# 32 unused bytes behind each tile of the split activations in a diffusion trunk layer

## The chip, the core and the metric

The kernel runs on one core of one Trainium2 chip. The metric is the time of one execution on the device in microseconds (us). The kernel before takes 2071.98 us, the median of two runs (2070.9 and 2073.06).

The core has engines that run side by side: TensorE (PE; its weight loads are shown apart as PEld), VectorE (DVE), ScalarE (ACT), GpSimd (POOL) and SyncE (SP), whose queue here issues most of the transfers. TensorE multiplies a stationary operand, which a weight load brings in first, with a moving operand that streams past it column by column. Both operands come from SBUF, the on-chip memory of 128 partitions; a tile's address is the same byte offset in each partition. Products land in PSUM, from where the other engines read them.

## The reference

One layer of a diffusion backbone for 128 context tokens and 256 latent tokens, d = 2048, float32:

```python
def trunk_layer(x, cond, lw, attend):
    sh1, sc1, g1, sh2, sc2, g2 = modulation(cond, w_mod_l, b_mod_l)
    h = rms_norm(x, n1) * (1 + sc1) + sh1
    q, k, v, u = project_in(h, w_in_l, qg_l, kg_l)      # 2048 x 4096
    attn = attend(q, k, v)
    x = x + g1 * token_mixing(h, attn, u, w_na_proj_l, w_fnet_proj_l, w_gate_l, w_o_l)
    h2 = rms_norm(x, n2) * (1 + sc2) + sh2
    x = x + g2 * swiglu(h2, w_gu_l, w_down_l)           # 2048 x 11264, 5632 x 2048
    return x, k, v

def token_mixing(h, attn, u, w_na_proj, w_fnet_proj, w_gate, w_o):
    na = attn.reshape(b, t, D_NA) @ w_na_proj
    fn = fourier_mix(u) @ w_fnet_proj
    g_na, g_fn = jnp.split(jax.nn.sigmoid(h @ w_gate), 2, axis=-1)
    return (g_na * na + g_fn * fn) @ w_o
```

Context tokens attend to context tokens; latent tokens attend to a window of their grid and to a cached context. The outputs are the new tokens of both kinds and the context's keys and values.

## The kernel before, in words

**Precision by three products.** Every float32 operand x is split into two tiles of a faster float32 form: H, a rounded copy (ScalarE, line 137), and L = x - H (VectorE, line 138). `mm3` (lines 140 to 143) then adds three matmuls into one PSUM tile: aH with bH (line 141), aH with bL (line 142) and aL with bH (line 143). The first argument is stationary and the second moves.

**Weights** come in units of 256 rows by 512 columns (`load_unit`, line 178) in one long fixed order, `units`. `next_unit` splits the unit ahead into `wh` and `wl`, tiles of [128, 2, 512], so 4096 bytes in a partition, three buffers each in `wpool`. A matmul reads either 512 columns of such a tile as the moving operand or a slice of 128 columns (512 bytes) as the stationary one.

**Activations** lie transposed, with channels on the partitions and the 384 tokens along the free dimension: a tile of [128, 384] float32, 1536 bytes. `hH[kt]` and `hL[kt]`, kt = 0 to 15, are allocated by `new_h` in the pool `hpool`, one tag for each, in the order H0, L0, H1, L1 and so on. The same 32 places are used three times: for the modulated input h, for the mixed branches (`mixH`, `mixL`), and for the second normalised input. The feed-forward part is done in pieces of eight (at last four) tiles of hidden channels; `cH[i]` and `cL[i]`, i = 0 to 7, are the split products of silu(g) and a, of the same size, in the pool `actp`.

**The stages**, in order of time: the input projection (h stationary, weights move, 512 columns), with the modulation vectors computed alongside; the gates (weights stationary, h moves, 384 columns), with the Fourier branch and attention run in small steps between; the two branch projections (weights stationary; the branch tiles `aH`, `aL`, `fH`, `fL` move); the output projection (the mixed tiles stationary, 512 columns); then six times gate-and-up (h moves, 384 columns) and down (c stationary, 512 columns). Work that runs alongside is held in generators (`Paced`) that a fixed number of steps is taken from at each weight unit, so that the order on each engine is fixed by the program. The last results are added up and stored at the end of the last down projection.

**Two places that the prediction looks at besides.** In the Fourier branch, `channels` multiplies tables of cosines and sines (stationary) with the sums over positions, tiles of [128, 2, 2, 194] (`sums`), 388 moving columns in two groups of 194. In attention, `values` multiplies the values (stationary) with the transposed probabilities `pt`, 512 moving columns in two runs of 256, and then 256 for the context.

**Where tiles lie.** In the pool `small` one tile, `pad`, of 480 bytes is allocated and never used. In the program before, `hH`, `hL`, `cH`, `cL`, `wh`, `wl`, `aH`, `aL`, `fH` and `fL` all begin at 288 modulo 512.

Of the kernel before, what the change touches and what calls it, by code (L numbers as in the profile page):

```python
# [13 lines left out]
F32 = mybir.dt.float32  # L14
F32R = mybir.dt.float32r
# [4 lines left out]
P = 128  # L20
# [9 lines left out]
TOK = CTX + LAT  # L30
# [65 lines left out]
def trunk_kernel(ctx: ExitStack, tc: tile.TileContext, io: dict):  # L96
# [25 lines left out]
    hpool = ctx.enter_context(tc.tile_pool(name="hpool", bufs=1))  # L122
# [9 lines left out]
    def nm(s):  # L132
        return f"{s}{next(ids)}"


    def split(H, L, x):
        nc.scalar.copy(H, x)  # L137
        nc.vector.tensor_sub(L, x, fr(H))  # L138

    def mm3(out, aH, aL, bH, bL, start, stop):  # L140
        nc.tensor.matmul(out, aH, bH, start=start, stop=False)  # L141
        nc.tensor.matmul(out, aH, bL, start=False, stop=False)  # L142
        nc.tensor.matmul(out, aL, bH, start=False, stop=stop)  # L143
# [58 lines left out]
    def next_unit(late=False):  # L202

        for p in front:
            p.tick()
        if not late:
            split_unit()
        for p in front + behind:
            p.tick()
        loads.more()  # L210
        return ready.popleft()
# [12 lines left out]
    hH = [None] * KT  # L224
    hL = [None] * KT

    def new_h(kt):
        hH[kt] = hpool.tile([P, TOK], F32R, tag=f"tH{kt}", name=nm(f"hH{kt}_"))
        hL[kt] = hpool.tile([P, TOK], F32R, tag=f"tL{kt}", name=nm(f"hL{kt}_"))
        return hH[kt], hL[kt]  # L230

    s_qkvu = [dram.tile([P, NT, CH], F32, tag=f"sq{i}", name=f"s_qkvu{i}") for i in range(8)]
# [28 lines left out]
    with ExitStack() as ph:  # L261
# [12 lines left out]
        def acc_tile():  # L274

            return next(ring)()
# [146 lines left out]
        with ExitStack() as pha:  # L423
# [90 lines left out]
            def modulate(kt):  # L514
                o = at_tile()
                for t in range(NT):
                    x = xc[kt // 4][:, t, kt % 4 * P : (kt % 4 + 1) * P]
                    if kt < 4:
                        nc.tensor.matmul(o[:, t * P : (t + 1) * P], x, diag[:, t], start=True, stop=True)
                    else:  # L520
                        nc.tensor.transpose(o[:, t * P : (t + 1) * P], x, ident)
                H, L = new_h(kt)
                f = tmp.tile([P, TOK], F32, tag="hf", name=nm("hf"))
                if kt == 0:
                    for cnd, sl in ((0, slice(0, CTX)), (1, slice(CTX, TOK))):
                        sc, sh = (m[0][:, kt, cnd : cnd + 1] for m in (msc, msh))
                        nc.vector.tensor_scalar(f[:, sl], o[:, sl], sc, sh, op0=ALU.mult, op1=ALU.add)
                        nc.scalar.copy(H[:, sl], f[:, sl])
                        nc.vector.tensor_sub(L[:, sl], f[:, sl], fr(H[:, sl]))
                    return  # L530
                for cnd, sl in ((0, slice(0, CTX)), (1, slice(CTX, TOK))):
                    nc.scalar.activation(
                        out=f[:, sl], in_=o[:, sl], func=AF.Identity,
                        scale=msc[0][:, kt, cnd : cnd + 1], bias=msh[0][:, kt, cnd : cnd + 1],
                    )
                split(H, L, f)
# [476 lines left out]
        def mixed(f4, gl):  # L1013
            for f in range(4):
                kt = f4 * 4 + f
                mixH[kt], mixL[kt] = new_h(kt)
                nc.vector.tensor_add(gl[0][:, f], gl[0][:, f], gl[1][:, f])
                split(mixH[kt], mixL[kt], gl[0][:, f])
                if f == 3:
                    gates.more()  # L1020
                    gates.more()
                yield
# [156 lines left out]
    def split_act(i, sg, cH, cL):  # L1179
        for f in range(4):  # L1180
            split(cH[i + f], cL[i + f], sg[:, f])
            yield

    def gated():

        rows_until(5)
        phr.close()
        pool = phr.enter_context(tc.tile_pool(name="gbp", bufs=1, side="right"))
        for cc in range(4):
            yield from load_rows(pool, 5, cc)  # L1190
        for cc in range(4):
            for t in range(NT):
                v = facc[cc][:, t]
                nc.vector.tensor_mul(v, v, gb[cc][:, min(t, 1)])
                nc.vector.tensor_add(x2[cc][:, t], x2[cc][:, t], v)
                yield

    f0 = 0
    for part, nf in enumerate(FF_PARTS):
        last = part == len(FF_PARTS) - 1  # L1200
        if last:
            behind.append(Paced(gated(), 1.5))
        cH = [None] * nf
        cL = [None] * nf
        for c4 in range(nf // 4):
            for half in (1, 0):
                po = [acc_tile() for _ in range(4)]
                for u in range(0, KT, 2):
                    wH, wL = next_unit()
                    if u == KT - 2 and facc is None:  # L1210
                        norm.drain()
                        rows.rate = RATES[4]
                        pho.close()
                        actp = phf.enter_context(tc.tile_pool(name="actp", bufs=1))
                        facc = [actp.tile([P, NT, CH], F32, tag=f"fa{i}", name=f"facc{i}") for i in range(4)]
                        ftmp = phf.enter_context(tc.tile_pool(name="tmpf", bufs=2))
                    for f in range(4):
                        s = slice(f * P, (f + 1) * P)
                        for kk in range(2):
                            k = u + kk  # L1220
                            mm3(po[f][:, :TOK], wH[:, kk, s], wL[:, kk, s], hH[k], hL[k], k == 0, k == KT - 1)
                        if u < KT - 2:
                            continue
                        if half:
                            if f == 0:
                                sg = ftmp.tile([P, 4, TOK], F32, tag="sg", name=nm("sg"))
                            nc.scalar.activation(out=sg[:, f], in_=po[f][:, :TOK], func=AF.Silu)
                        else:
                            i = c4 * 4 + f
                            nc.vector.tensor_mul(sg[:, f], sg[:, f], po[f][:, :TOK])  # L1230
                            cH[i] = actp.tile([P, TOK], F32R, tag=f"cH{i}", name=nm("cH"))
                            cL[i] = actp.tile([P, TOK], F32R, tag=f"cL{i}", name=nm("cL"))
                            if nf == 4:
                                split(cH[i], cL[i], sg[:, f])
            if nf > 4:
                behind.append(Paced(split_act(c4 * 4, sg, cH, cL), 2))
        for cc in range(4):
            po = [acc_tile() for _ in range(NT)]
            for u in range(0, nf, 2):
                wH, wL = next_unit()  # L1240
                for t in range(NT):
                    sl = slice(t * P, (t + 1) * P)
                    for kk in range(2):
                        k = u + kk
                        mm3(po[t], cH[k][:, sl], cL[k][:, sl], wH[:, kk], wL[:, kk], k == 0, k == nf - 1)
                    if u < nf - 2:
                        continue
                    if part == 0:
                        nc.scalar.copy(facc[cc][:, t], po[t])
                    elif not last:  # L1250
                        nc.vector.tensor_add(facc[cc][:, t], facc[cc][:, t], po[t])
                    else:
                        d = ftmp.tile([P, CH], F32, tag="d", bufs=1, name=nm("d"))
                        nc.vector.tensor_mul(d, po[t], gb[cc][:, min(t, 1)])
                        nc.vector.tensor_add(x2[cc][:, t], x2[cc][:, t], d)
                        y = yp if t == 0 else ys[(t - 1) * P : t * P]
                        nc.sync.dma_start(y[:, cc * CH : (cc + 1) * CH], x2[cc][:, t])
        f0 += nf
# [52 lines left out]
```

## Time and profile before

| | before |
|---|---|
| median of the runs | 2071.98 us (2070.9 to 2073.06) |
| the profiled execution's own time | 2074.18 us |
| its span, first to last instruction | 2072.4 us |
| mean granted TensorE clock | 0.997 |
| instructions | 27373 |
| moved by DMA | 390.45 MB, mean 188 GB/s |

The profile comes from one execution. Its rows of groups give line, engine, operation, the tile written and the tiles read, the shape, the number of instructions, then after the bar the busy time in us and the mean of one in ns, and then the idle time just before them with what ended it. A row of the list of waits gives who waited for whom, then the total in us, the number of times and the longest. A row of the timeline gives the start in us from the span's start, the duration in us, and the instruction. Matmuls are pipelined and their ends are modelled: their durations overlap, so that the distance from one start to the next, and not the duration, is what a matmul costs when TensorE is the limit.

### The profile page before, as it was taken

What the parts mean: (1) busy time and instruction counts of PE and PEld (TensorE: products, weight loads), DVE (VectorE), ACT (ScalarE), POOL (GpSimd) and SP (SyncE); (2) the same over time, 40 slices, a digit from 0 to 9 for tenths busy, and PEclk for the clock granted to TensorE, in tenths of its full rate; (3) what the DMA queues carried; (4) which work ended last, traced back from release to release, by engine and by line L of the source; (5) the groups of instructions that cost most, each with busy time, mean ns of one, the idle gap of its engine ahead of it and who ended that gap; (6) DMA issues with size and microseconds to landing.
All of it is one profiled execution on the core that took longest, in us unless ns stands there. A gap on an engine that the chain in (4) does not pass through costs nothing.

```text
span 2072.4 us, 27373 instructions
## 1 busy us (share of the span) xinstructions
PE 2036.6 (98%) x10963; PEld 1847.0 (89%) x10963; DVE 1209.9 (58%) x1418; ACT 756.2 (36%) x1146; POOL 58.0 (3%) x101
## 2 busy tenths in 40 slices
PE   6999999999999999998999999999999999999999
PEld 4668888999999999887998899899989998999897
DVE  4634899687885787765554444544454434333456
ACT  5323232456665433334433332223222232223222
POOL 3000000000001000001000000000000000000000
PEclk9999999999999999999999999999999999999999
DMA  9886878677674766654455454455454444444453
GB/s 336 286 321 211 295 254 309 211 212 235 212 218 152 261 230 212 235 191 128 150 161 159 157 162 148 138 162 157 158 158 137 123 132 124 130 125 130 128 167 122
DMA packets 219999, 390.45 MB, mean 188 GB/s; under 512 B 28080, under 2 KB 64960, under 8 KB 219872
## 3 DMA queue, kind: packets, MB, share of 16 engines
q1 hardware_dynamic: 212704, 382.13, 58.1%
q10 hardware_dynamic: 4672, 6.31, 0.8%
q8 instruction: 86, 1.41, 0.3%
q0 software_dynamic: 2496, 0.27, 0.1%
q14 instruction: 41, 0.34, 0.0%
HBM read 371.81 MB, written 20.51 MB: 189 GB/s over the span
## 4 chain that ended last, share of the span: by engine, by line
PE 94%; DVE 2%; DMA 1%; ACT 1%; issue 1%; SPq 1%; ACTq 0%; DVEq 0%
PE mm L141 19%; PE mm L142 19%; PE mm L143 19%; PE at L143 11%; PE at L141 11%; PE at L142 11%; PE md L390 1%; DMA wm<-in_w_mod 1%; DVE accr L314 1%; PE at L850 1%; PE at L918 1%; DVE wl L138 1%; DMA xc<-in_x_sample 0%; SPq L368 0%; PE md L324 0%
## 5 line engine op out<-in xcount | busy, mean ns | idle before, releaser
L138 DVE TENSOR_TENSOR wl<-wraw,wh 128x1024 fp32r<-128x1024 f32 (+1 forms) x464 | 559.4, 1206 | 703.3 <-ACT wh L137 702.2
L137 ACT CAST wh<-wraw 128x1024 fp32r<-128x1024 f32 (+1 forms) x464 | 480.7, 1038 | 1034.0 <-PE at L142 293.1
L141 PE MATMUL mm<-hH,wh 128*128 128x384 f32 x1216 | 411.5, 338 | 4.0 <-ACT gst L984 2.3
L143 PE MATMUL mm<-hH,wl 128*128 128x384 f32 x1216 | 407.3, 335 | 0.0
L142 PE MATMUL mm<-hL,wh 128*128 128x384 f32 x1216 | 407.1, 335 | 0.0
L314 DVE SCALAR_TENSOR_TENSOR accr<-wmr,csz,accr 128x1024 f32<-128x1024 f32 x240 | 304.8, 1278 | 0.0
L141 PE MATMUL at<-hH,wh 128*128 128x384 f32 x704 | 236.3, 336 | 1.4 <-ACT hH L1156 1.4
L141 PEld LDWEIGHTS mm<-hH,wh 128*128 128x128 f32 x1216 | 228.9, 188 | 9.6 <-ACT gst L984 3.5
L142 PE MATMUL at<-hL,wh 128*128 128x384 f32 x704 | 236.2, 336 | 0.0
L143 PE MATMUL at<-hH,wl 128*128 128x384 f32 x704 | 235.7, 335 | 0.0
L142 PEld LDWEIGHTS mm<-hL,wh 128*128 128x128 f32 x1216 | 229.0, 188 | 0.0
L143 PEld LDWEIGHTS mm<-hH,wl 128*128 128x128 f32 x1216 | 228.7, 188 | 0.0
L141 PE MATMUL mm<-wh,hH 128*128 128x512 f32 x431 | 172.7, 401 | 0.0
L142 PE MATMUL mm<-wl,hH 128*128 128x512 f32 x431 | 168.7, 391 | 1.7 <-DVE wl L138 1.7
L143 PE MATMUL mm<-wh,hL 128*128 128x512 f32 x431 | 168.3, 391 | 0.0
L143 PE MATMUL mm<-wh,cL 128*128 128x512 f32 x352 | 137.1, 389 | 0.0
L141 PE MATMUL mm<-wh,cH 128*128 128x512 f32 x352 | 137.0, 389 | 0.0
L142 PE MATMUL mm<-wl,cH 128*128 128x512 f32 x352 | 137.0, 389 | 0.0
L141 PEld LDWEIGHTS at<-hH,wh 128*128 128x128 f32 x704 | 132.6, 188 | 2.8 <-ACT hH L1156 1.8
L142 PEld LDWEIGHTS at<-hL,wh 128*128 128x128 f32 x704 | 132.6, 188 | 1.1 <-DVE hL L1162 0.7
L143 PEld LDWEIGHTS at<-hH,wl 128*128 128x128 f32 x704 | 132.6, 188 | 0.0
L141 PEld LDWEIGHTS mm<-wh,hH 128*128 128x128 f32 x431 | 81.2, 188 | 31.0 <-issue 9.8
(240 smaller groups left out, 2383.0 us busy)
## 6 DMA issues: line engine op xcount, KB each, us to landing
wraw<-in_w_gate_up SPq DMA_DIRECT2D x176, 512.0 KB, 3.7
wmr<-in_w_mod SPq DMA_DIRECT2D x128, 512.0 KB, 4.2
wraw<-in_w_down SPq DMA_DIRECT2D x88, 512.0 KB, 3.7
wm<-in_w_mod SPq DMA_DIRECT2D x64, 512.0 KB, 6.9
wraw<-in_w_gate SPq DMA_DIRECT2D x64, 512.0 KB, 5.0
wraw<-in_w_in SPq DMA_DIRECT2D x56, 512.0 KB, 5.9
wraw<-in_w_o SPq DMA_DIRECT2D x32, 512.0 KB, 5.4
wraw<-in_w_fnet_proj SPq DMA_DIRECT2D x16, 512.0 KB, 6.1
```

The costliest lines, as they stand in the source:

```text
L137: nc.scalar.copy(H, x)
L138: nc.vector.tensor_sub(L, x, fr(H))
L141: nc.tensor.matmul(out, aH, bH, start=start, stop=False)
L142: nc.tensor.matmul(out, aH, bL, start=False, stop=False)
L143: nc.tensor.matmul(out, aL, bH, start=False, stop=stop)
L314: nc.vector.scalar_tensor_tensor(out=acc[:, cnd], in0=wm, scalar=sc, in1=acc[:, cnd], op0=ALU.mult, op1=ALU.add)
L390: nc.tensor.matmul(pm[q : q + 32, :w], csz[:, k, :], wm[:, ty, kk + par, :], start=k < 2, stop=k >= KT - 2, tile_position=(0, q), skip_gro ...
L850: nc.tensor.matmul(po[j][:, cols], qx[rows[j], q], kx[rows[j], k], start=i == 0, stop=i == 2, tile_position=(j * HD, 0),)
L918: nc.tensor.transpose(o[:, i * P : (i + 1) * P], sc[:, j, c0 : c0 + P], ident)
```

## The change

Behind each h tile and each c tile, when it is first allocated, one tile of [128, 8] float32 is allocated with a tag of its own. It takes 32 bytes in each partition and is neither written nor read. The pitch of the tiles grows from 1536 to 1568 bytes. The name given to the c tiles is changed as well, which has no effect on the program.

```diff
     hH = [None] * KT
     hL = [None] * KT
 
+    def spread(pool, n):
+
+        pool.tile([P, 8], F32, tag=f"gap{n}", bufs=1, name=f"gap{n}")
+
     def new_h(kt):
+        new = hH[kt] is None
         hH[kt] = hpool.tile([P, TOK], F32R, tag=f"tH{kt}", name=nm(f"hH{kt}_"))
+        if new:
+            spread(hpool, f"H{kt}")
         hL[kt] = hpool.tile([P, TOK], F32R, tag=f"tL{kt}", name=nm(f"hL{kt}_"))
+        if new:
+            spread(hpool, f"L{kt}")
         return hH[kt], hL[kt]
...
-                            cH[i] = actp.tile([P, TOK], F32R, tag=f"cH{i}", name=nm("cH"))
-                            cL[i] = actp.tile([P, TOK], F32R, tag=f"cL{i}", name=nm("cL"))
+                            cH[i] = actp.tile([P, TOK], F32R, tag=f"cH{i}", name=nm(f"cH{i}_"))
+                            if part == 0:
+                                spread(actp, f"H{i}")
+                            cL[i] = actp.tile([P, TOK], F32R, tag=f"cL{i}", name=nm(f"cL{i}_"))
+                            if part == 0:
+                                spread(actp, f"L{i}")
```

## The prediction

> **What bounds the kernel now.** I read the page's first and fourth parts, then the list of what TensorE waited for, then three stages by window, then TensorE's groups by shape.
>
> ```profile
> span 2072.4 us, 27373 instructions
> PE 2036.6 (98%) x10963; PEld 1847.0 (89%) x10963; DVE 1209.9 (58%) x1418; ACT 756.2 (36%) x1146; POOL 58.0 (3%) x101
> PE 94%; DVE 2%; DMA 1%; ACT 1%; issue 1%; SPq 1%; ACTq 0%; DVEq 0%
> ```
>
> TensorE is busy for 98% of the span and is 94% of the chain that ended last. The two longest of its waits, and the one on a weight split, are small:
>
> ```profile
> PE at L519 <- DVE diag L508: 8.2, 1, 8.2
> PE at L465 <- DMA rows_c<-in_c: 6.2, 1, 6.2
> ...
> PE mm L142 <- DVE wl L138: 1.7, 3, 0.8
> ```
>
> So what counts is how fast one matmul follows another. A busy share can't tell that, because matmuls overlap; a window that holds a known number of starts can. The columns are window, length, busy time of PE with its instructions, granted clock, DMA share, GB/s.
>
> ```profile
> 690.00:823.00 133.00, 133.00 (x770) 1.00 0.71 242
> 1171.49:1304.55 133.06, 133.06 (x769) 1.00 0.50 155
> 1106.23:1171.49 65.26, 65.26 (x289) 1.00 0.52 161
> ```
>
> The second window is one gate-and-up stage: 768 matmuls of 384 columns start in it (the 769th began before), so one takes 133.06/768 = 173.3 ns. The third is one down projection: 288 matmuls of 512 columns, 226.6 ns each. The difference over 128 columns is 0.4167 ns a column; what is left is 173.3 - 384 x 0.4167 = 13.3 ns in both. Each matmul thus costs its columns plus 13.3 ns, at a full granted clock and with nothing waited for. This fixed part is what the change can touch.
>
> ```profile
> L141 PE MATMUL mm<-hH,wh 128*128 128x384 f32 x1216 | 411.5, 338 | 4.0 <-ACT gst L984 2.3 <-DVE acc L640 1.7
> L141 PE MATMUL at<-hH,wh 128*128 128x384 f32 x704 | 236.3, 336 | 1.4 <-ACT hH L1156 1.4
> L141 PE MATMUL mm<-wh,hH 128*128 128x512 f32 x431 | 172.7, 401 | 0.0
> L141 PE MATMUL mm<-wh,cH 128*128 128x512 f32 x352 | 137.0, 389 | 0.0
> L141 PE MATMUL at<-wh,cH 128*128 128x512 f32 x176 | 68.6, 390 | 0.0
> L141 PE MATMUL at<-wh,hH 128*128 128x512 f32 x145 | 56.8, 392 | 0.0
> ```
>
> Lines 142 and 143 have as many each. The matmuls that read a moved tile are 3 x (1216 + 704) = 5760 of 384 columns, where the h tile streams past (gates, gate-and-up), and 3 x (431 + 145 + 352 + 176) = 3312 of 512 columns, where an h or c tile is the loaded weight (input projection, output projection, down projection): 9072 of 10963.
>
> **What the change does, part by part.** It adds no instruction, no wait and no transfer: the 32-byte tiles are never read or written. Nothing passes another thing in a queue. The tiles of h grow from 1536 = 3 x 512 bytes to a pitch of 1568, so their remainders modulo 512 go from one value to sixteen: H of k-tile k moves by 64k, L by 64k + 32. The 32 gaps of h add 1024 bytes and the 16 of c add 512, both multiples of 512, so all that lies behind them keeps its remainder. Weight tiles are 4096 bytes and the slices of them 512 bytes apart, so they too keep one remainder, the same one as h has now (288 in the program's allocation). No DMA touches h or c.
>
> ScalarE and VectorE write these tiles at new addresses. The rows of the feed-forward part:
>
> ```profile
> L138 DVE TENSOR_TENSOR wl<-wraw,wh 128x1024 fp32r<-128x1024 f32 x263 | 322.1, 1225 | 562.7 <-ACT wh L137 562.7
> ...
> L138 DVE TENSOR_TENSOR cL<-sg,cH 128x384 fp32r<-128x384 f32 x44 | 22.6, 552 | 2.3 <-ACT cH L137 2.3
> ...
> L137 ACT CAST cH<-sg 128x384 fp32r<-128x384 f32 x44 | 20.5, 510 | 5.0 <-DVE sg L1230 5.0
> ```
>
> I cost that at nothing. Even a tenth on 22.6 and 20.5 us is 4 us, and VectorE idles 562.7 us there in front of its weight splits, under matmuls; without that cover it would be those 4 us.
>
> What is left is the 13.3 ns. Between two matmuls TensorE loads the next weights while the present columns stream, both out of SBUF, and the change alters where the two reads stand to each other. The trace of before has places where this relation differs. **Nearest**, the channel transform of the Fourier branch: the same three-product helper, 388 columns, whose moving tiles are 2 x 2 x 194 x 4 = 3104 = 6 x 512 + 32 bytes, so AH0, AL0, AH1, AL1 stand 0, 32, 64 and 96 bytes apart modulo 512 (16 more in their second half), while its weights keep one remainder.
>
> ```profile
> 432.09 0.34 PE L141 MATMUL at<-AH,chanH 128*128 128x388 f32 x1
> ...
> 434.03 0.34 PE L143 MATMUL at<-AH,chanL 128*128 128x388 f32 x1
> 434.21 0.33 PE L141 MATMUL mm<-hH,wh 128*128 128x384 f32 x1
> ```
>
> Twelve start in 2.12 us: 176.7 ns, less 388 x 0.4167 = 161.7 leaves 15.0 ns, **1.7 more** than 13.3. Second, the values product of attention, 512 columns in two pieces, all at the one remainder, but between other shapes:
>
> ```profile
> 468.68 0.39 PE L141 MATMUL at<-pt,v 128*128 128x512 f32 x1
> ...
> 470.76 0.28 PE L141 MATMUL at<-pt,v 128*128 128x256 f32 x1
> 470.87 0.28 PE L142 MATMUL at<-pt,v 128*128 128x256 f32 x1
> 470.99 0.28 PE L143 MATMUL at<-pt,v 128*128 128x256 f32 x1
> 471.11 0.34 PE L141 MATMUL mm<-hH,wh 128*128 128x384 f32 x1
> ```
>
> Nine of 512 in 2.08 us are 231.1 ns, **4.5 more** than 226.6; the three of 256 take 0.35/3 = 116.7 ns, **3.3 less** than 256 x 0.4167 + 13.3 = 120.0. Third, the first matmuls after a break, at unchanged remainders:
>
> ```profile
> 461.78 0.33 PE L142 MATMUL mm<-hL,wh 128*128 128x384 f32 x1
> ...
> 462.85 0.33 PE L142 MATMUL mm<-hL,wh 128*128 128x384 f32 x1
> 463.02 0.33 PE L143 MATMUL mm<-hH,wl 128*128 128x384 f32 x1
> ```
>
> ```profile
> 127.53 0.39 PE L142 MATMUL mm<-wl,hH 128*128 128x512 f32 x1
> ...
> 128.92 0.39 PE L142 MATMUL mm<-wl,hH 128*128 128x512 f32 x1
> 129.15 0.39 PE L143 MATMUL mm<-wh,hL 128*128 128x512 f32 x1
> ```
>
> Six take 1.07 us, 178.3 ns or **5.0 more**; six of 512 take 1.39 us, 231.7 ns or **5.1 more**; then the steady pace returns. I read this as a rhythm: with all remainders equal and all lengths multiples of 512 bytes, every matmul meets the next load in the same way, and the pace settles within some six matmuls at 13.3 ns. Different remainders change that meeting at every matmul, so the pace can't settle at one value.
>
> The bounds for one matmul are therefore -3.3 ns (the 256-column rows) and +5.1 ns (the unsettled rows). For the 384-column products I take +1.7, since the channel transform has nearly their shape and, like them, a spread stream against fixed weights. For the 512-column ones, where the weight side is spread, I take +4.5, the row of that length at an unsettled pace. The sum:
>
> - 5760 x 1.7 ns = 9.8 us
> - 3312 x 4.5 ns = 14.9 us
>
> together **24.7 us**. All of it reaches the end, because TensorE is the chain. Only in the input projection is another engine near enough to absorb some (VectorE is busy 87 of 100 us there), which I don't deduct:
>
> ```profile
> 200.00:300.00 100.00, 100.00 (x445) 81.89 (x445) 87.07 (x97) 30.09 (x33) 4.38 (x9) 1.00 0.85 288
> ```
>
> The profiled execution took 2074.18 us around its span of 2072.4; with the sum 2098.9. It lies 2.2 us over the median of the runs, 2071.98, so for the median I predict **2097 us**, 1.2% slower.
>
> **The rivals.** *Nothing changes.* If the extra time in the three places comes from what precedes them (other shapes, a pattern in two pieces, a break) and not from addresses, the steady pace stays at 173.3 and 226.6 ns, and the time at 2072. For it: the two strongest excesses are at equal remainders. Against it: the twelve channel matmuls follow one another without a break and don't settle. That the gaps are not laid out at all would end at 2072 too.
>
> The Trainium skill, "TensorE: Matmul & The Clock Gate", section "Step-by-step: what each phase is for", gives TensorE two independent read ports and says that loading the next weights takes no read bandwidth from the running matmul; by that rule this rival is right. The trace speaks against it only with the channel rows, 15.0 against 13.3 ns.
>
> *Slower by over 2%.* The pace never settles: every matmul pays what the first six after a break pay, 5760 x 5.0 + 3312 x 5.1 = 45.7 us, 2118 us. It decides from 2% = 41.4 us on, a mean of 4.6 ns a matmul. For it: those rows have the kernel's own shapes. Against it: the nearest spread case shows 1.7.
>
> *Faster.* Equal remainders might be the bad case, with both reads starting in the same place each time, and spreading them would avoid part of the 13.3 ns, as the 256-column rows do: 9072 x 3.3 = 30 us off, 2042 us; over 2% it needs 4.6 ns. For it: 13.3 ns on every matmul is much to lose. Against it: the channel transform is spread and no faster. The same page, section "Wait — 56ns, not 53.3ns?", gives columns over 2.4 GHz plus about 2.5 ns for back-to-back matmuls; by it 10.8 of the 13.3 ns could go at best, some 98 us. No row here shows such a pace.
>
> **How the numbers follow.** The forecast, a loss between 0.5 and 4.5 ns a matmul (5 to 41 us), gets 0.57; nothing changes, 0.18; slower by over 2%, 0.17; faster, 0.08, half of it beyond 2%. Two per cent is about what a measurement of this kernel can tell from no change. So faster 0.04, same 0.79, slower 0.17. The range runs from 2067 (no change, and half a nanosecond won on each) to 2120 (the unsettled pace everywhere, and 2 us of spread between runs).
>
> **What would show it.** Right: the same instructions and waits; the gate-and-up window of 133.06 us longer by 768 x 1.7 = 1.3 us, the down projection of 65.26 us by 288 x 4.5 = 1.3 us; the mean durations in the groups above up by like amounts. The stage at 690 to 823 us (its a and f tiles are not spread) must stay at 133.0 us: if it moves too, addresses are not the cause. Wrong: windows of the old length, or the loss in VectorE, ScalarE or a DMA wait instead of in matmul pace.

## The result, and the profile after

| | before | after |
|---|---|---|
| median of the runs | 2071.98 us | 2092.26 us (2091.62 to 2092.89) |
| span of the profiled execution | 2072.4 us | 2089.8 us |
| mean granted TensorE clock | 0.997 | 0.998 |

The ratio is 1.0093, with a 95% interval of 1.0076 to 1.011: the change costs 20.3 us, 16 to 23 us by the interval. It is a real loss, but smaller than 2%. The forecast was 2097 us.

The first and fourth parts of the page of after, and then the same three rows of its list of waits, answer to the rows of before in the prediction:

```profile
span 2089.8 us, 27373 instructions
PE 2055.2 (98%) x10963; PEld 1851.0 (89%) x10963; DVE 1211.2 (58%) x1418; ACT 755.4 (36%) x1146; POOL 57.6 (3%) x101
...
PE 94%; DVE 2%; DMA 2%; ACT 1%; issue 1%; SPq 1%; ACTq 0%; DVEq 0%
```

```profile
PE at L528 <- DVE diag L517: 8.0, 1, 8.0
PE at L474 <- DMA rows_c<-in_c: 5.9, 1, 5.9
...
PE mm L142 <- DVE wl L138: 0.8, 2, 0.6
```

Every engine has the same number of instructions, and none of the three waits shown is longer. Two of the shorter ones have grown, by 1.0 and 0.3 us (the weights of the modulation and the second normalised input); all waits of TensorE in the list take 29.9 us together, where they took 31.1. TensorE's busy time has grown by 18.6 us and the span by 17.4; VectorE's and ScalarE's have moved by about 1 us. The new tiles are written at the old price. The groups of after (columns as in the prediction):

```profile
L138 DVE TENSOR_TENSOR wl<-wraw,wh 128x1024 fp32r<-128x1024 f32 x263 | 322.3, 1226 | 573.3 <-ACT wh L137 573.3
...
L138 DVE TENSOR_TENSOR cL<-sg,cH 128x384 fp32r<-128x384 f32 x44 | 22.6, 553 | 2.3 <-ACT cH L137 2.3
...
L137 ACT CAST cH<-sg 128x384 fp32r<-128x384 f32 x44 | 20.5, 508 | 5.0 <-DVE sg L1239 5.0
```

So the time went into the pace of matmuls. The window view, now cut at the first and the last start of each stage (window, length, busy time of PE with its instructions, granted clock, DMA share, GB/s), gives four stages of before: the branch projections, the output projection, one gate-and-up and one down.

```profile
690.05:824.40 134.35, 134.35 (x777) 1.00 0.71 243
824.40:968.46 144.06, 138.37 (x629) 0.99 0.57 190
1171.51:1304.65 133.14, 133.14 (x769) 1.00 0.50 155
1106.19:1171.51 65.32, 65.32 (x290) 1.00 0.52 161
```

And the same four of after:

```profile
692.83:827.18 134.35, 134.35 (x777) 1.00 0.71 243
827.18:973.24 146.06, 140.22 (x628) 1.00 0.57 187
1178.96:1312.83 133.87, 133.87 (x769) 1.00 0.49 154
1112.09:1178.96 66.87, 66.87 (x289) 1.00 0.51 158
```

The branch projections, whose tiles did not move, take exactly what they took: 134.35 us. Their start is 2.78 us later, which is the net loss of all that comes before them, the input projection and the gates. The output projection loses 2.0 us. A down projection loses 1.55 us, 1.55/288 = 5.4 ns a matmul. A gate-and-up stage loses 0.73 us, 0.73/768 = 0.95 ns a matmul. There are 5.5 of each of these two (five pieces of eight tiles and one of four), so the down stages lose 8.5 us and the gate-and-up stages 4.0 us. The four amounts add up to 17.3 us, which is the span's 17.4.

TensorE's groups of after, kept apart by shape:

```profile
L141 PE MATMUL mm<-hH,wh 128*128 128x384 f32 x1216 | 416.1, 342 | 3.7 <-ACT gst L993 2.2 <-DVE acc L649 1.5
L142 PE MATMUL mm<-hL,wh 128*128 128x384 f32 x1216 | 408.6, 336 | 0.0
L143 PE MATMUL mm<-hH,wl 128*128 128x384 f32 x1216 | 407.0, 335 | 0.0
...
L141 PE MATMUL mm<-wh,cH 128*128 128x512 f32 x352 | 138.5, 394 | 0.0
...
L141 PE MATMUL at<-wh,hH 128*128 128x512 f32 x145 | 57.3, 395 | 0.0
```

The means rise from 338 to 342 ns in the first row and from 389 to 394 in the fourth; the rows of lines 142 and 143 with an h tile stay at 336 and 335, where they were 335 each. A mean duration shows that something moved, not how much: these records overlap. What a matmul costs is the distance from its start to the next one. Summed over all products with a moved tile, from the starts in the two traces, those distances are:

| | before | after | each |
|---|---|---|---|
| 5760 of 384 columns | 1012.5 us | 1016.1 us | +0.6 ns |
| 3312 of 512 columns | 762.5 us | 777.1 us | +4.4 ns |

### The profile page after: what moved, and what is told of

Read it like the earlier page. It is cut to its first block, busy times and chain, and to the rows that moved or that the text cites. A ratio compares the mean times of both kernels' runs of the same rounds, so it can differ in the third digit from the quotient of the medians.

```text
span 2089.8 us, 27373 instructions
## 1 busy us (share of the span) xinstructions
PE 2055.2 (98%) x10963; PEld 1851.0 (89%) x10963; DVE 1211.2 (58%) x1418; ACT 755.4 (36%) x1146; POOL 57.6 (3%) x101
## 4 chain that ended last, share of the span: by engine, by line
PE 94%; DVE 2%; DMA 2%; ACT 1%; issue 1%; SPq 1%; ACTq 0%; DVEq 0%
PE mm L141 20%; PE mm L142 19%; PE mm L143 19%; PE at L141 11%; PE at L142 11%; PE at L143 11%; DMA wm<-in_w_mod 1%; PE md L399 1%; DVE accr L323 1%; PE at L859 1%; PE at L927 1%; DMA xc<-in_x_sample 0%; DVE wl L138 0%; PE md L333 0%; SPq L377 0%
## 5 line engine op out<-in xcount | busy, mean ns | idle before, releaser
L141 PE MATMUL mm<-hH,wh 128*128 128x384 f32 x1216 | 416.1, 342 | 3.7 <-ACT gst L993 2.2
```

## Experiments

The theory that the result suggests is D, the **difference**: what a matmul costs above its columns is decided by how far, in remainder, the tile that streams lies from the stationary tile that is loaded meanwhile. The first rival is R, the prediction's **rhythm**: a difference costs only because it changes from matmul to matmul, and any constant one settles at 13.3 ns. The other rivals come with the runs that they belong to. All windows below are of the stages of the preceding section, or of parts of them. A changed kernel's time given without an interval is that of a single execution. The code cuts are shortened: long lists are written as products.

**One half of the change at a time.** In one kernel the 32 bytes lie only behind h, in the other only behind c.

```diff
 h_only: bytes behind each tile, in the order H0, L0, H1, L1, ...
+    H_GAPS = [32] * 32
+    C_GAPS = [0] * 16
 c_only:
+    H_GAPS = [0] * 32
+    C_GAPS = [32] * 16
```

> Only the 32 h tiles get their 32 bytes; the c tiles stay at one remainder. Theory A (each matmul that reads a spread tile pays on its own, by its shape): the trace after the whole change shows the 384-column products with h up by 3.6 us in all and the 512-column ones that load h up by 7.5 us, so 2072 + 11 = 2083 us, and the down projections at their old 226.6 ns. Rival B (the loss is one effect of the two together, or sits in one of them): near 2072 or near 2092 us.

> Only the 16 c tiles get their 32 bytes. Theory A: the down projections cost 1584 matmuls x 4.4 ns = 7 us more, 2079 us, and everything else keeps its pace, gate-and-up at 173.3 ns. Rival B: near 2072 or near 2092 us.

Measured, beside 2072.59 us for the kernel before: h_only 2083.79 us, ratio 1.0054 (1.0039 to 1.0069); c_only 2080.88 us, ratio 1.0041 (1.0026 to 1.0056). The gate-and-up and the down stage of h_only:

```profile
1178.13:1311.98 133.85, 133.85 (x769) 1.00 0.49 154
1112.83:1178.13 65.30, 65.30 (x290) 1.00 0.50 161
```

and of c_only:

```profile
1172.85:1305.99 133.14, 133.14 (x770) 1.00 0.49 155
1105.97:1172.85 66.88, 66.88 (x290) 1.00 0.50 157
```

Each stage is slow exactly where its own tiles were moved, by the same amount as in the whole change within 0.02 us, and untouched, within the same 0.02 us, where they were not. The two halves, 11.2 and 8.3 us, add up to 19.5 of the 20.3.

**Which remainder counts.** All H stay, all L go 256 bytes further modulo 512. (Where a cut below sets `H_AT` and `L_AT`, every tile of h and c is laid out once ahead of its first use, with gap tiles that bring it to its remainder.)

```diff
+    H_AT = [0] * 16
+    L_AT = [256] * 16
+    CH_AT = [0] * 8
+    CL_AT = [256] * 8
+    lay(hpool, "h", 0, [(f"tH{k}", H_AT[k]) for k in range(KT)] + [(f"tL{k}", L_AT[k]) for k in range(KT)])
...
+                        lay(actp, "c", 0, [(f"cH{i}", CH_AT[i]) for i in range(8)] + [(f"cL{i}", CL_AT[i]) for i in range(8)])
```

> All H tiles keep the old remainder and all L tiles stand 256 bytes past it modulo 512, so the remainders modulo 512 alternate from one matmul to the next. Theory P256 (the trace after the change shows the same pace for remainders that differ by 256, so only the remainder modulo 256 counts): nothing changes, 2072 us within 2 us, 173.3 and 226.6 ns. Rival P512 (any change of remainder modulo 512 from one matmul to the next breaks the settled pace): slower, by up to the 20 us of the whole change.

Measured 2073.54 us, ratio 1.0002 (0.9993 to 1.0012). Its gate-and-up and down stages:

```profile
1170.80:1303.94 133.14, 133.14 (x769) 1.00 0.50 155
1105.48:1170.80 65.32, 65.32 (x290) 1.00 0.51 161
```

These two stages don't change, to a hundredth of a microsecond, though H and L lie 256 bytes apart. So a shift by 256 counts as none. The trace after the change shows the same at other remainders: there the places of k-tiles 4 and 5 differ by 256 bytes from those of 8 and 9, and in one gate-and-up stage the distances from start to start in their weight units go 15, 14, 10, 16, 19, 15, 14, 17, 12 and 15, 14, 10, 17, 18, 15, 15, 16, 13 ns above the columns, alike to the 1 ns of the records. The remainder that counts is the one modulo 256, and the sixteen remainders modulo 512 that the prediction names are eight that differ.

**A constant difference.** All tiles of h and c go 64 bytes further; none is spread. In a second kernel 64 unused bytes at the end of the constants shift all that is allocated behind them, h, c and weights together.

```diff
 shift64:
+    H_AT = L_AT = [64] * 16
+    CH_AT = CL_AT = [64] * 8
 all_shift64:
+            consts.tile([P, 16], F32, tag="gap", name="gap")
```

> All h and c tiles stand 64 bytes past their old remainder, all alike, so that nothing is spread and the difference to the weight tiles is 64 at every matmul. Theory D (a constant difference has a settled pace of its own, as the scan showed): 384 columns stay at 13.3 ns over the columns, 512 columns go to the 20.0 ns of the scan, 3312 x 6.7 = 22 us, 2094 us, more than the whole spread cost. Theory R (only a changing difference costs): 2072 us.

> 64 bytes at the end of the constants, so that h, c, the weight tiles and all tiles behind them move together by 64 bytes modulo 512 and every difference is as before. Theory D (only the difference between the streamed tile and the tile loaded meanwhile counts): 2072 us within 2 us, 173.3 and 226.6 ns. Rival (the place itself counts, not the difference): the 512-column stages as in the kernel with h and c alone shifted, 2094 us.

Measured, beside 2072.84 us before: shift64 2091.07 us, ratio 1.0086 (1.0071 to 1.0101); all_shift64 2072.53 us, ratio 0.9997 (0.9988 to 1.0007). The gate-and-up and the down stage of shift64:

```profile
1181.57:1314.70 133.13, 133.13 (x769) 1.00 0.50 155
1114.38:1181.57 67.19, 67.19 (x289) 1.00 0.49 157
```

and of all_shift64:

```profile
1171.32:1304.46 133.14, 133.14 (x769) 1.00 0.50 155
1106.00:1171.32 65.32, 65.32 (x290) 1.00 0.51 161
```

Moving everything together costs nothing, so it is the difference between two tiles that counts and not a place. And a difference of 64 that never changes costs the down stage 1.87 us, 6.5 ns a matmul, more than the spread tiles do, while the 384-column stage keeps its 133.13 us. R fell: no change from matmul to matmul is needed to lose time. D's own figure was missed by a little, 2094 us expected against 2091.07: in front of the gates, where 1152 matmuls load h tiles, the kernel lost 4.0 us, and 1152 x 6.5 ns would be 7.5. Why the price is not paid in full there was not tested.

**The price of every difference.** In scan_same the k-tiles stand in pairs at 0, 32, ... 224 bytes past the old remainder, with H and L of a k-tile alike; the c tiles in pairs at 0, 64, 128 and 192. One weight unit then runs at one difference.

```diff
+    H_GAPS = [0, 0, 0, 32] * 8
+    C_GAPS = [0, 0, 0, 64] * 4
```

> H and L of k-tiles 0 and 1 keep the old remainder, those of 2 and 3 stand 32 bytes past it, and so on up to 224 bytes for 14 and 15; for c steps of 64 bytes by pairs. Within one weight unit (24 matmuls of 384 columns or 18 of 512) the difference between the moving and the loaded operand is then constant. Theory R (rhythm: what costs is that the difference changes from matmul to matmul): after the first few matmuls of each unit the pace settles at the old 13.3 ns over the columns at every difference; in all some 2 ns a matmul from the first ones, 2072 to 2090 us. Rival D (the difference itself has a price): each pair of k-tiles has a settled pace of its own, 13.3 ns only for the first pair, others between 8 and 20 ns, and some may be cheaper than 13.3 ns.

Measured 2090.68 us. Units of 24 matmuls of 384 columns at the differences 128, 160, 192, 224 and then 0, 32, 64, 96 (at 13.3 ns each they would take 24 x 173.3 = 4.16 us):

```profile
1194.92:1199.15 4.23, 4.23 (x26) 1.00 0.45 128
1199.15:1203.38 4.23, 4.23 (x25) 1.00 0.43 120
1203.38:1207.58 4.20, 4.20 (x26) 1.00 0.27 103
1207.58:1211.76 4.18, 4.18 (x25) 1.00 0.89 274
1211.76:1215.95 4.19, 4.19 (x26) 1.00 0.35 110
1215.95:1220.11 4.16, 4.16 (x26) 1.00 0.51 139
1220.11:1224.27 4.16, 4.16 (x25) 1.00 0.30 110
1224.27:1228.51 4.24, 4.24 (x26) 1.00 0.86 268
```

Eighteen matmuls of 512 columns at 0, 64, 128 and 192 (at 13.3 ns, 4.08 us):

```profile
1128.42:1132.50 4.08, 4.08 (x20) 1.00 0.34 120
1132.50:1136.69 4.19, 4.19 (x19) 1.00 0.69 216
1136.69:1140.88 4.19, 4.19 (x19) 1.00 0.55 174
1140.88:1145.00 4.12, 4.12 (x19) 1.00 0.43 132
```

In the first fence, the 4.19 of difference 0 comes from its first six matmuls, behind the jump from 224; then it runs at 13.3 ns. Read from the single starts, each difference settles in a pattern of its own in this run, in ns above the columns:

| difference | 384 columns | 512 columns |
|---|---|---|
| 0 | 13.3 | 13.3 |
| 32 | 13.3 | |
| 64 | 13.3 | 17 and 22.7 in turn, mean 20 |
| 96 | 14, 20, 15, 17.5, mean 16.7 | |
| 128 | 14, 15, 21.5, 16, 14, mean 16 | a cycle of seven, mean 19 |
| 160 | 14 and 19 in turn, mean 16.7 | |
| 192 | 17, 11, 17.5, 14, 13, mean 14.7 | mean 15.6 |
| 224 | 13.3 | |

The two prices at 64 that shift64 shares with this table agree: 13.3 for 384 columns, and 13.3 + 6.5 for 512. The length of every whole cycle, its columns included, is a multiple of 6.67 ns within the 1 ns of the records; 6.67 ns is the time of 16 columns (16 x 0.4167).

The two columns of the table can't be compared row by row. With 384 columns the shifted tile is the one that streams, with 512 it is the one that is loaded, so the stream lies ahead of the load in the one case and behind it in the other. Taken with its sign modulo 256, 64 at 384 columns answers to 192 at 512. No run separates the length from the role that the shifted tile has.

**Is there a pair under 13.3 ns?** In scan_L0 and scan_L32 H stays at a difference of 0 or 32 while L runs through all eight (c: H at 64 or 192, L through 0 to 192); in scan_A and scan_B the three buffers of low weights also get places of their own, 64, 128 and 192 or 32, 96 and 160 past the high ones.

```diff
 scan_L0:
+    H_AT = [0] * 16
+    L_AT = [32 * (k // 2) for k in range(16)]
 scan_L32:
+    H_AT = [32] * 16
+    L_AT = [32 * (k // 2) for k in range(16)]
 scan_A (scan_B: 32, 64, 64):
+    W_GAPS = [64, 64, 64, 320]
...
-            L = wpool.tile([P, 2, CH], F32R, tag="wl", name=nm("wl"))
+            if b not in placed:
+                wpool.tile([P, W_GAPS[b] // 4], F32, tag=f"gapw{b}", bufs=1, name=f"gapw{b}")
+            L = wpool.tile([P, 2, CH], F32R, tag=f"wl{b}", bufs=1, name=nm("wl"))
```

> H tiles keep the old remainder, L tiles of k-tiles 0 and 1 too, those of 2 and 3 stand 32 bytes past it, and so on to 224 for 14 and 15. For c, H stands at 64 and L at 0, 64, 128, 192 by pairs. Theory D with two parameters (difference of H to the high weight tile, of L to the low one): each pair of k-tiles has a settled cycle of its own whose sum over the cycle is a multiple of 6.67 ns, and the mean lies between 10 and 20 ns over the columns; one or more of the eight may lie under 13.3 ns. Rival (13.3 ns is the floor of a settled pace): none under 13.3 ns over a whole unit.

> As the scan before, with H of h at 32 past the old remainder and L of h at 0 to 224 by pairs of k-tiles; for c, H at 192 and L at 0, 64, 128, 192 by pairs. Theory D: settled cycles between 10 and 20 ns, the pair with L at 32 (equal remainders) at 13.3 ns for 384 columns. Rival: none under 13.3 ns over a whole unit.

> H and L of h stand at 0 to 224 by pairs of k-tiles as in the first scan; the three buffers of the low weight tile stand at 64, 128 and 192, so that each pair of k-tiles meets three differences of L and low weight. c at 0, 64, 128, 192 by pairs. Theory D: 24 combinations with settled cycles between 11 and 21 ns over the columns; slower than before in all by 15 to 30 us. Looked for: a combination under 13.3 ns for both lengths; the sums by 6.67 ns allow 11.1 or 12.2. Rival (13.3 ns is the floor): none.

> As the scan before with the low weight buffers at 32, 96 and 160: 24 more combinations. The same theories: cycles between 11 and 21 ns, 15 to 30 us slower in all; or none under 13.3 ns.

Measured 2094.3, 2095.82, 2098.56 and 2098.49 us. Over all five scans, and counted by two differences (of H to the high weight tile, of L to the low one, modulo 256), these are 58 combinations for 384 columns and, where more than 12 distances were left to read, 46 for 512 (down and output projections), the first two triples of every unit left out. None has a mean under 13.3 ns. For 384 columns eight stand at 13.3, some in an even pace and some in a cycle of uneven steps; the highest is 17.8. For 512 the lowest is 13.5 (all at 0), the next 15.8, the highest 21.9. In scan_L0, with H at 0 and L at 0 to 224, 384 columns cost 13.4, 15.6, 13.8, 16.7, 15.6, 15.6, 15.6 and 14.4 ns: H and L at 32 cost 13.3 together in scan_same, but L alone at 32 costs 15.6.

Nor has one combination a single price. Both at 32 took 13.3 ns in scan_same, and 16.6 in scan_L32, where the unit was entered from another neighbour and settled in a cycle of four (17, 15, 20, 14.5); the 13.3 ns expected for it there was missed. That the entry decides which cycle comes is a reading of these two runs and was not tested by itself. So the difference alone doesn't fix the price, and the table above holds for the order of scan_same.

The kernel before, with all remainders equal, stands at the lowest mean of all that was tried for both lengths, and no better layout was found among these.

**Does the price come from the length of the weight read?** Theory C, a guess that this run is to test: the time above the columns is made while the load reads its tile, so it goes with the number of weight columns. In half_scan the down projection loads only 64 of the 128 columns of c in the second and third products.

```diff
-                        mm3(po[t], cH[k][:, sl], cL[k][:, sl], wH[:, kk], wL[:, kk], k == 0, k == nf - 1)
...
+                        half = slice(t * P, t * P + 64)
+                        nc.tensor.matmul(po[t], cH[k][:, sl], wH[:, kk], start=k == 0, stop=False)
+                        nc.tensor.matmul(po[t][:64], cH[k][:, half], wL[:, kk], start=False, stop=False)
+                        nc.tensor.matmul(po[t][:64], cL[k][:, half], wH[:, kk], start=False, stop=False)
```

> Leaves out part of the down projection: in two of the three products (lines 142 and 143) only the first 64 of 128 columns of the c tile are loaded and only 64 of 128 output rows are added to, for all k-tiles but the last of each piece; h keeps its remainder, c stands at 0, 64, 128, 192 by pairs as in the first scan, where these four settled near 13.3, 20, 19 and 15.6 ns over the 512 columns. Theory C (the time over the columns is made where the streamed read meets the read of the next weights, so it goes with the length of that read): the matmuls during which a half tile is loaded (two of three) pay about half, 6 to 10 ns, and the four pairs differ less. Rival S (a fixed cost of switching weights, and addresses act in another way): the four paces of the first scan, 13.3 to 20 ns, on all three products.

Measured 2078.39 us, beside 2073.62 before. One down stage of half_scan:

```profile
1104.84:1171.18 66.34, 66.34 (x289) 1.00 0.51 159
```

and of scan_same, with the same places and whole loads:

```profile
1111.83:1178.18 66.35, 66.35 (x290) 1.00 0.50 159
```

A load of 64 columns is shorter in the records, 134 ns in place of 188, and yet the sum of the stage stays, so C fell. Single prices do move: a matmul during which a half tile was loaded cost 16.5 ns at difference 0 (13.4 at the same places in scan_same), 17.7 at 64 (20.0), 15.5 at 128 (19.8) and 16.4 at 192 (17.2). None comes near the 6 to 10 ns that C asked for; the rival S, the old four paces, isn't met either. That the sums agree to 0.01 us is therefore a balance of gains and losses.

**Does the length of the stream matter alike?** If the cycles come from 16-column steps, then a length that isn't a multiple of 16 must change the pace at unchanged remainders. In length_scan everything lies as before, and k-tiles 2 to 13 of gate-and-up stream only a part of their 384 columns. Rival F: a matmul costs its columns and 13.3 ns whatever the length.

```diff
+COLS = [384, 380, 376, 372, 368, 364, 360, 384]
...
-                            mm3(po[f][:, :TOK], wH[:, kk, s], wL[:, kk, s], hH[k], hL[k], k == 0, k == KT - 1)
+                            n = COLS[u // 2]
+                            mm3(po[f][:, :n], wH[:, kk, s], wL[:, kk, s], hH[k][:, :n], hL[k][:, :n], k == 0, k == KT - 1)
```

> Remainders as in the kernel before. Leaves out part of gate-and-up: k-tiles 2 to 13 stream only the first 380, 376, 372, 368, 364 and 360 of the 384 columns (by pairs of k-tiles), the first and last pair all of them. Theory G (the settled cycles close on a grid of 6.67 ns, which is 16 columns, so the price of a matmul depends on where its length ends on that grid): 368 columns cost 13.3 ns over their columns as 384 do, 376 cost another amount, near 10.0 or 16.7 ns in a settled pace or cycles whose mean is not 13.3. Rival F (13.3 ns is a fixed cost at equal remainders, whatever the length): 13.3 ns at all seven lengths, and the kernel 22 x 24 x 84 columns x 0.4167 ns = 18.5 us shorter, 2054 us.

Measured 2058.93 us, beside 2072.9 before; F said 2054. Units of 24 matmuls with 380, 376, 372, 368, 364 and 360 columns:

```profile
1204.96:1209.06 4.10, 4.10 (x26) 1.00 0.51 140
1209.06:1213.22 4.16, 4.16 (x26) 1.00 0.30 110
1213.22:1217.30 4.08, 4.08 (x26) 1.00 0.87 267
1217.30:1221.30 4.00, 4.00 (x26) 1.00 0.43 136
1221.30:1225.30 4.00, 4.00 (x26) 1.00 0.42 132
1225.30:1229.25 3.95, 3.95 (x26) 1.00 0.44 136
```

376 columns take the 4.16 us that 384 take at their settled pace, 364 the 4.00 us of 368. Settled, the means of whole cycles above the columns are 12.8 ns at 380, 16.7 at 376, 15.0 at 372, 13.3 at 368, 15.0 at 364 and 14.4 at 360. Again whole cycles close on multiples of 6.67 ns: two matmuls of 376 columns take 346.7 ns = 52 x 6.67, two of 372 take 340 = 51 x 6.67. F fell, and length alone can change the cycle. What the expectation said of 368, the even pace of 384, held in the mean only: its steps go 13.7, 14.7, 9.7, 15.7.

## Why the prediction was right, point by point

**What bounds, and by which view.** Right. The whole loss lies in the distance between matmul starts; the waits of TensorE did not grow in sum (29.9 us after 31.1), the other engines moved by about 1 us, and the stage whose tiles stayed (134.35 us twice) stayed. The writes at nothing were right too: 22.6 and 20.5 us are still 22.6 and 20.5.

**The 512-column term.** The number is right: 3312 x 4.5 = 14.9 us forecast, 14.6 us (4.4 ns each) measured. The row that it was taken from, nine matmuls of the values product, belongs to another case (equal remainders, after other shapes), so this closeness is luck: by stage the price is 5.4 ns in the down projection and 2.0 us / 576 = 3.5 ns in the output projection, about as much in the input projection (what is left of the 14.6 us, 4.1 over 1152 matmuls), and over single combinations the time above the columns goes from 13.5 to 21.9 ns. For the down projection the prediction asked for 1.3 us more in its window, and got 1.55.

**The 384-column term** is the step that was mis-sized: "For the 384-column products I take +1.7, since the channel transform has nearly their shape". Measured 0.6 ns over all 5760 and 0.95 ns in gate-and-up (0.73 us in the window where 1.3 was asked for): 3.6 us in place of 9.8. By the starts of all 5760, the distances from line 141 to the next grew by 3.0 ns and from line 142 by 0.5, while those from line 143 shrank by 1.6; a spread that also shortens some steps was not in the sum. And the nearest row was less near than it seemed: its 388 columns are no multiple of 16, and length_scan shows that a length can move the price by +3.3 ns (376) or -0.6 (380) with every remainder equal. How much of the channel transform's 1.7 ns was address and how much length wasn't measured; 388 was not run.

**The rhythm.** Half right. "Different remainders change that meeting at every matmul, so the pace can't settle at one value" has the right object, the way in which a stream meets the next load. But shift64 shows that a meeting which is always the same can be as dear (6.5 ns), and that the pace settles even so. In the changed kernel itself the gate-and-up units settle in a cycle of six matmuls, as 10, 13, 22, 14, 8 and 19 ns above the columns, mean 14.4. In its down units no cycle closes within the 18 matmuls; there the sentence holds as it stands. Loss needs differences that are dear, not a change of difference.

**The rivals.** "Nothing changes" fell to the result, 1.0076 to 1.011, and to h_only and c_only, whose slow stages are the moved ones. The Trainium skill's independent read ports ("TensorE: Matmul & The Clock Gate", section "Step-by-step: what each phase is for") don't explain shift64: 64 bytes of placement, with nothing else changed, cost 18.2 us. "Slower by over 2%" needed a mean of 4.6 ns a matmul; the 384-column products, the greater part, paid 0.6. "Faster" fell as far as it was tried: no spread of remainders, in 104 combinations (58 + 46), had a mean under 13.3 ns. The 2.5 ns over the columns that the Trainium skill gives in the section "Wait — 56ns, not 53.3ns?" of "TensorE: Matmul & The Clock Gate" were not reached by any settled pace of the three products; the smallest mean is the 12.8 ns at 380 columns.

**The size.** The measured interval, 16 to 23 us, ends a little below the forecast's 24.7. By the starts in the one pair of traces, 14.6 + 3.6 = 18.2 us of the 24.7 are there; of the missing 6.5 us, 6.2 are in the 384-column term.

**What stays open.** Which part of the chip makes a difference in remainder cost time. The price is not proportional to the load (half_scan), does not belong to a place (all_shift64), has a period of 256 bytes (l_at_256, and the units of the changed kernel), depends on how a unit is entered (both at 32), and moves in cycles whose sums are multiples of 6.67 ns. Two reads that take turns at the same SBUF on such a grid would fit, but no run here shows it.

## What to carry to other kernels

Where float32 matmuls of this kind run back to back with a new stationary tile each, start with the streamed tiles and the stationary ones at one remainder modulo 256 bytes; here 64 bytes more or less were worth 18 us of 2073. Before shortening a stream, measure the new length: 376 columns took as long as 384, and 364 as long as 368, while 380 and 368 saved at least the columns that they left out. An unused tile that pads a pool can cost a per cent though it adds no instruction: look at the remainders when an allocation changes. Measure this with windows of known numbers of starts, stage by stage; the busy share (98% in both kernels) can't show it.

## What the runs showed of the hardware that was not expected

- The period of 256 bytes: 256 bytes between H and L, 2073.54 us against 2072.59; 64 bytes, 2091.07 against 2072.84.
- Prices in cycles. A difference of 160 bytes gives 14 and 19 ns in turn, 96 bytes a cycle of four; each cycle is a multiple of 6.67 ns. In the kernel before, the starts of nearly all settled matmuls also lie close to one phase of a 6.67 ns grid in any 300 us, and that phase drifts by only some 3 ns from the first stage to the last.
- The same shift can be free in one stage and dear in another: 64 bytes cost nothing at 384 columns, where the shifted tile streams, and 6.5 ns at 512, where it is loaded.
- Fewer columns can take as long: 24 matmuls of 376 columns take 4.16 us, as 24 of 384 do.
